# A hybrid mixer and gated ConvFFN layer: the up projection by seven products for eight, the output projection by quarters of the tokens

## The chip, the cores and the metric

One core of one Trainium2 chip. The metric is the time on the device of one execution, in microseconds (us), as the median of the runs. The engines are called by their names in the profile: PE (matrix products; PEld its weight loads), DVE (vector), ACT (scalar functions), POOL (GpSimd), SP (the queue that issues the DMAs).

## What is computed

One layer of a decoder for T = 1056 tokens: a prompt of 1024 and 8 samples of 4. The mixer takes the normalised input through one input projection into three groups of heads, and their outputs through one output projection; then comes the gated ConvFFN, whose two projections are half of the work. D = 1024 features, D_FF = 2816.

```python
def conv_ffn(h, ffn_state, w_up, conv_w, conv_b, w_down):
    up = jnp.einsum('bld,df->blf', h, w_up)
    gate, val = up[..., :D_FF], up[..., D_FF:]
    gate, new_state = causal_dwconv(gate, ffn_state, conv_w, conv_b)   # width 3, over the tokens
    out = jnp.einsum('blf,fd->bld', jax.nn.gelu(gate, approximate=True) * val, w_down)
    return out, new_state.astype(ffn_state.dtype)

# in the layer
    mix, ... = hybrid_mixer(rms_norm(x, norm_mix_pre), ...)   # ends with einsum('ble,ed->bld', mix, w_out)
    x = x + rms_norm(mix, norm_mix_post)
    f, nf = conv_ffn(rms_norm(x, norm_ffn_pre), ...)
    x = x + rms_norm(f, norm_ffn_post)
```

## The kernel before

Features lie on the 128 partitions, tokens along the free dimension. A dense product of one output tile (128 features) with a group of tokens runs over k, the tiles of 128 input features. To keep float32 accuracy with the fp32r type of PE, each operand is split into a rounded part and the rest (`h` and `l`), and each k takes three matmuls: `wh` with `xh`, `wh` with `xl`, `wl` with `xh`. `dense` issues them (`mm`, L203 in the profile). The tokens are taken in NG = 3 groups of G = 352.

`load_w` brings a weight tile: the DMA on SP (L263), the rounded part by ACT (L264), the rest by a subtraction on POOL (L265).

The order of the work. Tile's scheduler orders DVE, ACT, POOL and SP by priority; PE's order is written by hand: the class `Weave` draws steps from several streams, and the next step is that of the first stream whose operands should be there.

The stages, with their place in the profiled execution:

- The mixer for the prompt, to about 641 us.
- The samples and the output projection, to 814.7 us. `split_mix` makes the split operands of the mixer's outputs; `project` forms the 8 output tiles, first the two groups 0 and 1 for as long as the streams of the samples last, then the rest, then group 2. `finish` adds the input to the normalised result and makes the split operands of the FFN.
- The up projection, in five parts of the hidden tiles (`QUARTERS`). For a hidden tile `gate_conv` makes the gate: 3 groups x 8 k x 3 matmuls, each group's sums scaled out of PSUM by DVE (L303), then the convolution: ACT takes the middle tap with the bias (L212), DVE the two other taps by `scalar_tensor_tensor` over 1072 columns (L1682), ACT the gelu. `value` does the other half (DVE L303, the product with the gate L1695 to L1699) and splits the result into `hidh` (ACT, L1700) and `hidl` (DVE, L1701), which stay in SBUF.
- After each part `down` multiplies its hidden tiles into all 8 output tiles and adds them to `fa` in SBUF (DVE, L1732 and L1734). The last part is taken by groups, so that `final` (the norm, the residual and the output, L1748 to L1758) of a group runs beside the products of the next.

In the FFN five PSUM banks take the products in turn. A weight tile is loaded into one buffer (`w`), its parts into two pairs.

## Time and profile before

| what | value |
|---|---|
| runs | 1576.37, 1582.40 and 1576.41 us, median 1576.41 |
| span of the profiled execution | 1578.6 us (its time outside the profiler is not listed) |
| PE busy | 1496.2 us, 95% of the span |
| DVE, ACT, POOL busy | 920.7, 542.1, 546.1 us |
| mixer, 0 to 640 us | PE busy 587 us |
| samples and output projection, 640 to 815 us | PE busy 164 us |
| up and down projections, 815 to 1510 us | PE busy 695 us, without a gap |
| last group and output, 1510 to 1578.6 us | PE busy 50 us |

The span is the time from the first to the last instruction that the profiler saw. Matmuls overlap in the profile: each is shown for about 0.32 us, but one starts every 0.16 us, so that a time per matmul is taken from the starts, or from a stretch without gaps divided by its matmuls. "Idle before" is what an engine waited before an instruction, and the name behind the arrow what released it.

### The profile page before, as it was taken

To read this page: it belongs to the slowest core of one execution; us is meant where nothing else is said; L and a number is where in the kernel's file an instruction comes from. 1 tells how busy PE (TensorE), PEld (TensorE's weight loads), DVE (VectorE), ACT (ScalarE), POOL (GpSimd) and SP (SyncE) were. 2 spreads that over 40 slices of the span, in tenths; PEclk is the share of its full clock that TensorE was granted. 3 is DMA by queue.
4 is the path that set the end of the run, shared out by engine and by line. 5 is a ranking of instruction groups with operands and counts; after the bars stand their busy time and mean duration, and the time that the engine had idled before them with its cause. 6 is when DMAs were issued, how large, how long until landed. Compare 5 with 4: busy or idle time off the path is not lost.

```text
span 1578.6 us, 24157 instructions
## 1 busy us (share of the span) xinstructions
PE 1496.2 (95%) x9438; PEld 1453.1 (92%) x9438; DVE 920.7 (58%) x1818; ACT 542.1 (34%) x1173; POOL 546.1 (35%) x624
## 2 busy tenths in 40 slices
PE   8788999989999999999899999999999999999995
PEld 8788899879989989988889999999999999999994
DVE  6889888796474367636975522444245325424558
ACT  7644445443342232424652211221122112212353
POOL 6234433232354353566432122221222222122224
PEclk9989999999999999999999999999999999999997
DMA  5111010111111231324531112111111111111142
GB/s 180 43 48 30 23 45 25 34 32 30 43 55 47 79 112 47 102 76 152 187 100 41 44 42 62 41 41 42 52 54 34 41 61 42 40 55 54 52 151 110
DMA packets 51210, 100.63 MB, mean 64 GB/s; under 512 B 14857, under 2 KB 25737, under 8 KB 50713
## 3 DMA queue, kind: packets, MB, share of 16 engines
q1 hardware_dynamic: 51096, 99.10, 20.1%
q8 instruction: 74, 1.21, 0.3%
q14 instruction: 40, 0.32, 0.1%
HBM read 85.25 MB, written 13.31 MB: 62 GB/s over the span
## 4 chain that ended last, share of the span: by engine, by line
PE 63%; DVE 17%; ACT 6%; POOL 5%; issue 4%; DMA 4%; SPq 0%; DVEq 0%; POOLq 0%; ACTq 0%
PE acc L203 55%; PE mc L203 3%; PE mb L203 3%; DVE kq L465 2%; PE mb L207 2%; DMA E<-rows_dram 2%; POOL wl L265 1%; DVE hl L333 1%; DVE two L784 1%; DVE v L465 1%; ACT sq L212 1%; POOL E L868 1%; PE po L203 1%; DVE fs L344 1%; ACT E L212 1%
## 5 line engine op out<-in xcount | busy, mean ns | idle before, releaser
L203 PE MATMUL acc<-hh,wh 128*128 128x352 f32 x1952 | 660.7, 339 | 18.2 <-DVE pre L303 12.2
L203 PE MATMUL acc<-hh,wl 128*128 128x352 f32 x1960 | 635.8, 324 | 2.6 <-POOL wl L265 2.0
L203 PE MATMUL acc<-hl,wh 128*128 128x352 f32 x1952 | 631.9, 324 | 0.7 <-DVE hl L333 0.7
L203 PEld LDWEIGHTS acc<-hh,wh 128*128 128x128 f32 x1952 | 371.7, 191 | 25.3 <-DVE pre L303 8.5
L265 POOL TENSOR_TENSOR wl<-w,wh 128x1024 fp32r<-128x1024 f32 (+2 forms) x117 | 252.9, 2162 | 362.3 <-ACT wh L264 354.8
L203 PEld LDWEIGHTS acc<-hh,wl 128*128 128x128 f32 x1960 | 372.4, 190 | 4.2 <-POOL wl L265 2.3
L203 PEld LDWEIGHTS acc<-hl,wh 128*128 128x128 f32 x1952 | 373.0, 191 | 3.1 <-DVE hl L333 1.7
L264 ACT CAST wh<-w 128x1024 fp32r<-128x1024 f32 (+2 forms) x117 | 109.9, 939 | 416.4 <-PE acc L203 400.3
L203 PE MATMUL acc<-hidh,wh 128*128 128x352 f32 x444 | 143.8, 324 | 0.0
L203 PE MATMUL acc<-hidh,wl 128*128 128x352 f32 x444 | 143.3, 323 | 0.0
L203 PE MATMUL acc<-hidl,wh 128*128 128x352 f32 x444 | 143.2, 322 | 0.0
L303 DVE TENSOR_TENSOR fpre<-acc,rs 128x352 f32<-128x352 f32 (+1 forms) x88 | 35.8, 430 | 137.5 <-PE acc L203 135.1
L1734 DVE TENSOR_TENSOR fa<-fa,acc 128x352 f32<-128x352 f32 x96 | 49.8, 519 | 106.3 <-PE acc L203 105.9
L1682 DVE SCALAR_TENSOR_TENSOR fy<-fpre,vec,fy 128x1072 f32<-128x1072 f32 x44 | 79.3, 1802 | 36.7 <-ACT fy L212 36.0
L203 PEld LDWEIGHTS acc<-hidh,wh 128*128 128x128 f32 x444 | 83.4, 188 | 0.0
L203 PEld LDWEIGHTS acc<-hidl,wh 128*128 128x128 f32 x444 | 83.4, 188 | 0.0
L203 PEld LDWEIGHTS acc<-hidh,wl 128*128 128x128 f32 x444 | 83.4, 188 | 0.0
L1701 DVE TENSOR_TENSOR hidl<-hid,hidh 128x352 fp32r<-128x352 f32 x66 | 52.7, 799 | 37.8 <-ACT hidh L1700 37.8
L1677 POOL COPY ffn_o<-fpre 128x2 f32<-128x2 f32 x22 | 4.1, 186 | 157.8 <-DVE fpre L303 157.8
L465 DVE SCALAR_TENSOR_TENSOR kq<-pre,cw,kq 128x352 f32<-128x352 f32 (+1 forms) x72 | 53.4, 748 | 7.7 <-ACT kq L212 7.2
L1700 ACT CAST hidh<-hid 128x352 fp32r<-128x352 f32 x66 | 31.9, 483 | 74.2 <-DVE hid L1695 49.9
L303 DVE TENSOR_TENSOR hid<-acc,rs 128x352 f32<-128x352 f32 x66 | 34.4, 521 | 38.1 <-PE acc L203 38.1
(552 smaller groups left out, 2238.7 us busy)
## 6 DMA issues: line engine op xcount, KB each, us to landing
w<-in_w_up_dram SPq DMA_DIRECT2D x44, 512.0 KB
w<-in_w_in_dram SPq DMA_DIRECT2D x30, 512.0 KB
E<-rows_dram SPq DMA_DIRECT2D x24, 256.0 KB
w<-in_w_dn_dram SPq DMA_DIRECT2D x21, 256.0 KB
w<-in_w_out_dram SPq DMA_DIRECT2D x10, 512.0 KB
w<-in_w_dn_dram SPq DMA_DIRECT2D x16, 320.0 KB
xr<-in_xT_dram SPq DMA_DIRECT2D x24, 176.0 KB
hh<-x_dram SPq DMA_DIRECT2D x3, 1408.0 KB
```

The source lines that it names most:

```text
L203: return nc.tensor.matmul(out, **kw)
L207: return nc.tensor.transpose(out, in_, identity)
L212: i = nc.scalar.activation(**kw)
L264: nc.scalar.copy(out=wh[:, ks], in_=w[:, ks])
L265: gtt(out=wl[:, ks], in0=w[:, ks], in1=wh[:, ks].bitcast(F32), op=ALU.subtract)
L303: vtt(out=out, in0=ps, in1=r, op=ALU.mult)
L333: stt(out=hl[g][:, k, :], in0=x, scalar=col(vcol + k), in1=hh[g][:, k, :].bitcast(F32), op0=ALU.mult, op1=ALU.subtract)
L465: stt(out=y[:, a:b], in0=pre[:, a + j:b + j], scalar=cw2[:, 4 * t + j:4 * t + j + 1], in1=y[:, a:b], op0=ALU.mult, op1=ALU.add)
L1682: stt(out=y[:, :LF], in0=pre[:, j:j + LF], scalar=col(V_FW + 3 * f + j), in1=y[:, :LF], op0=ALU.mult, op1=ALU.add)
L1700: nc.scalar.copy(out=hidh[:, groups[g]], in_=hid)
L1701: vtt(out=hidl[:, groups[g]], in0=hid, in1=hidh[:, groups[g]].bitcast(F32), op=ALU.subtract)
L1734: vtt(out=fa[:, g, m, :], in0=fa[:, g, m, :], in1=ps[:, :G], op=ALU.add)
```

## The change

The tokens of the output projection and of the FFN are taken in NQ = 4 quarters of Q = 264.

The up projection. Two gate tiles of a pair (or two value tiles) and two quarters of tokens, with the input features in two halves of KH = 4 tiles, are a product of 2 x 2 blocks. It is formed by seven block products instead of eight (Winograd's form). The input sums are built once (`pieces`, on DVE, with the split by ACT and DVE); the weight sums are built for each pair by four DVE operations of 128x512 (`weights`), and each of the seven weight pieces is split by ACT and by POOL, or by DVE for p = 2 and 4 (`weight_piece`). The class `fast` is one pair, a task: product p of the two-quarter halves u = 0 and 1 is 4 k x 3 matmuls of 264 columns each. Products that belong to the same output are summed in one PSUM bank (1 and 2; 6, 7 and 4; 5 and 3), and what is shared between banks goes through SBUF (`f1`, `f6`, `f7`, L1872 and L1875). In a task's order, products 4 and 3 of the pair before stand between this pair's product 6 of u = 0 and its product 5. The first PLAIN = 4 gate tiles are done by plain products, since the input sums are not ready yet. Tasks: the value tiles 0 and 1, then by turns a gate pair and the value pair before it; 20 tasks in all.

The hidden tiles are written to DRAM (`hid_dram`) and read back for the down projection (`load_hid`), which now comes after the whole up projection, in six parts (`PARTS`, the first of one hidden tile alone), by quarters of tokens. The output projection takes quarters 0 and 1 beside the samples (`project_first`) and 2 and 3 after them (`project_last`). The weight buffer `w` has three places. PE's order is by hand to the end. The buffers of the mixer's normalised input become 16 tiles `h0` to `h15` over all tokens.

```diff
-QUARTERS = ((0, 5), (5, 10), (10, 14), (14, 18), (18, 22))
+Q = 264
+NQ = 4
+PLAIN = 4
+PARTS = ((0, 1), (1, 6), (6, 10), (10, 14), (14, 18), (18, 22))
...
+        def project_first():
+            for m in range(KD):
                 w = load_w(I["w_out"][m], KD)
-                for g in range(2):
-                    yield from product(m, w, g)
-                m += 1
-            yield lambda: not weave.streams[1:]
+                for q in range(2):
+                    yield from product(m, w, q)
+            for q in range(2):
+                weave.add(finish(q), 8)
+            have.add("half")
...
+            split_mix(2)
+            for m in range(3):
+                load(m)
+            split_mix(3)
+            for q in (2, 3):
+                for m in range(KD):
+                    yield from product(m, held[m], q)
+                    if q == 2 and m + 3 < KD:
+                        load(m + 3)
+                    if q == 3 and m < PLAIN:
+                        load_up(m)
+                weave.add(finish(q), 8)
+            have.add("projected")
...
+            def split(p, x):
+                hi, lo = (block(pool.tile([P, T], F32R, name=n)) for pool, n in places[p])
+                nc.scalar.copy(out=hi, in_=x)
+                vtt(out=lo, in0=x, in1=hi.bitcast(F32), op=ALU.subtract)
+                X[u][p] = hi, lo
...
+        def gate_task(i):
+            pres = [new_pre() for j in range(2)]
+            def out(j, h, u, x, ps):
+                gate_in(pres[j], 2 * u + h, x, ps)
+            def end():
+                ys[i] = [gate_conv(2 * i + j, pres[j]) for j in range(2)]
+            return fast(i, 0, out, end)
...
+                if x is not None:
+                    t = fo[0].tile([P, Q], F32, name="rs", bufs=2)
+                    vtt(out=t, in0=x, in1=ps, op=ALU.add)
+                    ps = t
+                for a, b, smp in quarter(q):
+                    o, p_, y = hids[j][:, q * Q + a:q * Q + b], ps[:, a:b], ys[i][j][:, q * Q + a:q * Q + b]
+                    if smp:
+                        o, p_ = (t.rearrange("p (b t) -> p b t", t=DS) for t in (o, p_))
+                        y = samp6(ys[i][j], SEQ + 2)[:, :, 0:DS]
+                    vtt(out=o, in0=y, in1=p_, op=ALU.mult)
...
+                    dma(out=hid_dram[2 * i + j], in_=hids[j])
+                ys.pop(i)
...
+            wh, wl = ring.pop(0)
+            nc.scalar.copy(out=wh, in_=x)
+            tt(out=wl, in0=x, in1=wh.bitcast(F32), op=ALU.subtract)
+            return wh, wl
...
+        class fast:
+            def __init__(self, i, val, out, end):
+                self.out, self.end = out, end
+                w = [wp.tile([P, KD, P], F32, name="w", bufs=3) for j in range(2)]
+                self.A = [[w[j][:, KH * r:KH * r + KH] for j in range(2)] for r in range(2)]
+                for r, j in ((0, 0), (1, 0), (1, 1), (0, 1)):
+                    dma(out=self.A[r][j], in_=I["w_up"][2 * (2 * i + r) + val][:, KH * j:KH * j + KH])
+                self.banks, self.sb, self.w = {}, {}, {}
+            def weights(self, p):
+                A = self.A
+                if p == 6:
+                    self.s = [fo[0].tile([P, KH, P], F32, name="ws", bufs=3) for j in range(2)]
+                    vtt(out=self.s[0], in0=A[1][0], in1=A[1][1], op=ALU.add)
+                    vtt(out=self.s[1], in0=self.s[0], in1=A[0][0], op=ALU.subtract)
+                elif p == 7:
+                    vtt(out=A[1][0], in0=A[0][0], in1=A[1][0], op=ALU.subtract)
+                elif p == 3:
+                    vtt(out=self.s[1], in0=A[0][1], in1=self.s[1], op=ALU.subtract)
+                x = {1: A[0][0], 2: A[0][1], 4: A[1][1], 7: A[1][0]}.get(p)
+                if x is None:
+                    x = self.s[p != 5]
+                return weight_piece(x, vtt if p in (2, 4) else gtt)
+            def run(self, p, u):
+                if p not in self.w:
+                    self.w[p] = self.weights(p)
+                wh, wl = self.w[p]
+                first = p in (1, 6, 5)
+                b = {1: 0, 2: 0, 6: 1, 7: 1, 4: 1, 5: 2, 3: 2}[p]
+                if first:
+                    self.banks[u, b] = (accr if b else accp).tile([P, 512], F32, name="acc")[:, :Q]
+                ps = self.banks[u, b]
+                xh, xl = X[u][p]
+                for k in range(KH):
+                    kw = dict(skip_group_check=not first)
+                    mm(ps, lhsT=wh[:, k, :], rhs=xh[:, k, :], start=first and k == 0, stop=False, **kw)
+                    mm(ps, lhsT=wh[:, k, :], rhs=xl[:, k, :], start=False, stop=False, **kw)
+                    mm(ps, lhsT=wl[:, k, :], rhs=xh[:, k, :], start=False, stop=k == KH - 1, **kw)
+                    yield 0
+                sb = self.sb
+                if p == 1:
+                    sb[u, 1] = fo[0].tile([P, Q], F32, name="f1", bufs=3)
+                    nc.scalar.copy(out=sb[u, 1], in_=ps)
+                elif p in (6, 7):
+                    sb[u, p] = fo[0].tile([P, Q], F32, name=f"f{p}", bufs=3 if p == 6 else 2)
+                    vtt(out=sb[u, p], in0=sb[u, 1], in1=ps, op=ALU.add)
+                    if p == 7:
+                        self.out(1, 1, u, sb[u, 7], self.banks[u, 2])
+                elif p == 2:
+                    self.out(0, 0, u, None, ps)
+                elif p == 4:
+                    self.out(1, 0, u, sb[u, 1], ps)
+                elif p == 3:
+                    self.out(0, 1, u, sb[u, 6], ps)
...
+            for q in range(NQ):
+                yield lambda: ("normed", q) in have
+                for f in range(PLAIN):
+                    ps = yield from dense(accr, held["up", f], operand, KD, q, Q)
+                    gate_in(pres[f], q, None, ps)
+                have.add(("plain", q))
...
+            prev = None
+            for n, (task, i) in enumerate(tasks):
+                cur = task(i)
+                if n == 0:
+                    for i in range(PLAIN // 2):
+                        ys[i] = [gate_conv(2 * i + j, pres[2 * i + j]) for j in range(2)]
+                for p, u in ((1, 0), (1, 1), (6, 0), (4, 0), (6, 1), (4, 1), (3, 0), (3, 1),
+                             (5, 0), (5, 1), (2, 0), (2, 1), (7, 0), (7, 1)):
+                    if p in (4, 3):
+                        if prev:
+                            yield from prev.run(p, u)
+                            if (p, u) == (3, 1):
+                                prev.end()
+                    else:
+                        yield from cur.run(p, u)
+                prev = cur
...
+        def load_hid(f, parts):
+            h, l = parts
+            dma(out=l.bitcast(F32), in_=hid_dram[f])
+            nc.scalar.copy(out=h, in_=l.bitcast(F32))
+            vtt(out=l, in0=l.bitcast(F32), in1=h.bitcast(F32), op=ALU.subtract)
+            return parts
...
+        for qi, (f0, f1) in enumerate(PARTS):
+            nf = f1 - f0
+            n = KD if qi == 0 else KD // nf
+            after = []
+            todo = list(range(PARTS[qi + 1][1] - f1)) if qi < last else []
+            if qi < last:
+                for m in range(KD):
+                    if m % n == 0:
+                        ws = first if qi == 0 else down_w(qi, m, n)
+                    for q in range(NQ):
+                        down(m, ws[m % n], q, qi, hid)
+                        if todo and (qi == 0 or q == 0):
+                            after.append(new_hid(qi + 1, todo.pop(0)))
+                hid = after
```

### How the order moves

PE, one pair of the up projection. Names: `hh0` to `hh2` are the operands of the three groups. Before, one tile takes its 24 matmuls for group 0, then those for groups 1 and 2, each group into a bank of its own:

```order
L203 MATMUL acc_10588<-hh0_7760,wh_10583 128x352
L203 MATMUL acc_10588<-hl0_7761,wh_10583 128x352
L203 MATMUL acc_10588<-hh0_7760,wl_10584 128x352
...
L203 MATMUL acc_10618<-hh1_7904,wh_10583 128x352
...
L203 MATMUL acc_10648<-hh2_8178,wh_10583 128x352
```

Now, in a gate task in the middle of the up projection, the first matmul of each of its first eight products (p,u), which are (1,0), (1,1), (6,0), then (4,0) of the pair before, (6,1), then (4,1), (3,0) and (3,1) of the pair before; 11 more matmuls follow each:

```order
L206 MATMUL acc_10596<-h0_7826,wh_10547 128x264
...
L206 MATMUL acc_10611<-h8_8325,wh_10547 128x264
...
L206 MATMUL acc_10634<-n0_8409,wh_10630 128x264
...
L206 MATMUL acc_10380<-n6_8522,wh_10630 128x264
...
L206 MATMUL acc_10666<-r0_8647,wh_10630 128x264
...
L206 MATMUL acc_10412<-h4_8738,wh_10630 128x264
...
L206 MATMUL acc_10492<-h5_7900,wh_10697 128x264
...
L206 MATMUL acc_10505<-h13_8605,wh_10697 128x264
```

Of the five banks `accr`, four are held by the pair before and `acc_10634` is the fifth; `acc_10666` is the bank that `acc_10380` leaves. Behind the products shown come (5,0), (5,1), (2,0), (2,1), (7,0) and (7,1), then the next task.

DVE, the convolution of a gate. Before, it stands between the sums of its own tile and those of the next, value tile (`rs` are the norm's factors):

```order
L303 TENSOR_TENSOR fpre_13556<-acc_13559,rs0_8079 128x352
L303 TENSOR_TENSOR fpre_13556<-acc_13585,rs1_8166 128x352
L303 TENSOR_TENSOR fpre_13556<-acc_13611,rs2_8257 128x320
L303 TENSOR_TENSOR fpre_13556<-acc_13611,rs2_8257 128x8x4
L1682 SCALAR_TENSOR_TENSOR fy_13640<-fpre_13556,vec_75,fy_13640 128x1072 x2
L303 TENSOR_TENSOR hid_13678<-acc_13653,rs0_8079 128x352
L1695 TENSOR_TENSOR hid_13678<-fy_13545,hid_13678 128x352
L1701 TENSOR_TENSOR hidl0_13646<-hid_13678,hidh0_13645 128x352
```

Now two gates' convolutions (four operations: both gates' first taps, then both second) stand between the outputs of product 3 and of product 2, and the next task's first weight sums (`ws`) behind the outputs of products 2 and 7:

```order
L1773 SCALAR_TENSOR_TENSOR fy_11454<-fpre_11078,vec_75,fy_11454 128x1072
L1773 SCALAR_TENSOR_TENSOR fy_11463<-fpre_11079,vec_75,fy_11463 128x1072
...
L1805 TENSOR_TENSOR n10_8895<-fy_10962,acc_11328 128x264
L1805 TENSOR_TENSOR n10_8895<-fy_10962,acc_11343 128x264
L1875 TENSOR_TENSOR f7_11547<-f1_11341,acc_11364 128x264
L1841 TENSOR_TENSOR ws_11610<-w_11572,w_11573 128x512
L1798 TENSOR_TENSOR rs_11549<-f7_11547,acc_11476 128x264
L1875 TENSOR_TENSOR f7_11564<-f1_11356,acc_11396 128x264
L1805 TENSOR_TENSOR n11_8896<-fy_10971,rs_11549 128x264
L1798 TENSOR_TENSOR rs_11566<-f7_11564,acc_11489 128x264
L1842 TENSOR_TENSOR ws_11611<-ws_11610,w_11572 128x512
```

What moved: four long operations together instead of two, with the weight sums queued on the same engine behind the outputs that follow.

DVE, the first part of the down projection. Before, its copies from PSUM (`fa`) follow the hidden tiles that DVE just made, with nothing else between them:

```order
L1697 TENSOR_TENSOR hid_9246<-fy_9049,hid_9246 128x320
L1699 TENSOR_TENSOR hid_9246<-fy_9049,hid_9246 128x32
L1701 TENSOR_TENSOR hidl4_9154<-hid_9246,hidh4_9153 128x352
L1732 COPY fa_9252<-acc_9259 128x352
```

Now the first part's 32 copies have the splits of the next part's five reloaded hidden tiles between them:

```order
L1798 TENSOR_TENSOR rs<-f_13629,acc 128x264
L1805 TENSOR_TENSOR n_8893<-fy,rs 128x232
L1805 TENSOR_TENSOR n_8893<-fy,rs 128x32
L1967 COPY fa<-acc 128x264 x12
L1946 TENSOR_TENSOR hidl_13880<-hidl_13880,hidh_13879 128x1056
L1967 COPY fa<-acc 128x264
L1946 TENSOR_TENSOR hidl_13890<-hidl_13890,hidh_13889 128x1056
L1967 COPY fa<-acc 128x264
L1946 TENSOR_TENSOR hidl_13900<-hidl_13900,hidh_13899 128x1056
```

What moved: the products of one hidden tile alone (32 groups of 3 matmuls) stand before those that need five reloaded tiles.

## Rows read from the trace of the kernel before

**Rows 1.** Windows by stage: us, PE, PEld, DVE, ACT, POOL busy, PEclk, DMA share, GB/s.

```profile
core 0 of [0], span 1578.6 us
...
760.00:815.00 55.00, 45.56 (x238) 42.27 (x238) 47.99 (x79) 32.61 (x68) 20.40 (x16) 0.91 0.46 147
815.00:1510.00 695.00, 695.00 (x4350) 695.00 (x4350) 296.53 (x445) 150.06 (x189) 165.20 (x165) 1.00 0.16 51
...
1558.00:1579.00 21.00, 2.79 (x5) 1.12 (x4) 16.28 (x24) 3.22 (x6) 9.74 (x9) 0.56 0.36 137
```

**Rows 2.** Chain of waits, its longest piece: start us, us, what.

```profile
814.71 694.66 PE acc L203 x4344
```

**Rows 3.** Waits of PE, 760 to 815 us: us in total, times, longest.

```profile
PE acc L203 <- ACT mix L1571: 3.3, 1, 3.3
PE acc L203 <- POOL wl L265: 2.0, 1, 2.0
...
PE acc L203 <- ACT wh L264: 1.0, 1, 1.0
```

**Rows 4.** Timeline of PE's weight loads where products are short: start us, us.

```profile
682.27 0.41 PEld L203 LDWEIGHTS mc<-kqG,hh 128*128 128x128 f32 x3 [0.24 <-issue]
...
682.60 0.19 PEld L203 LDWEIGHTS acc<-hh,wh 128*128 128x128 f32 x1
```

**Rows 5.** Lines by form, 900 to 1500 us: busy us, mean ns, idle before.

```profile
L1682 DVE SCALAR_TENSOR_TENSOR fy<-fpre,vec,fy 128x1072 f32<-128x1072 f32 x34 | 62.8, 1846 | 27.8 <-ACT fy L212 27.2
...
L303 DVE TENSOR_TENSOR hid<-acc,rs 128x352 f32<-128x352 f32 x51 | 26.6, 521 | 31.9 <-PE acc L203 31.9
...
L265 POOL TENSOR_TENSOR wl<-w,wh 128x512 fp32r<-128x512 f32 x17 | 23.2, 1366 | 85.8 <-ACT wh L264 85.8
L212 ACT ACTIVATE fy<-fpre,vec 128x1072 f32<-128x1072 f32 x17 | 21.8, 1281 | 0.0
...
L264 ACT CAST wh<-w 128x512 fp32r<-128x512 f32 x17 | 10.6, 621 | 65.2 <-PE acc L203 65.2
...
L303 DVE TENSOR_TENSOR fpre<-acc,rs 128x320 f32<-128x320 f32 x17 | 8.4, 492 | 56.2 <-PE acc L203 56.2
```

**Rows 6.** Timeline of all engines, a bank's release in the mixer.

```profile
50.48 0.32 PE L203 MATMUL acc<-hh,wl 128*128 128x352 f32 x1
...
50.83 0.51 DVE L303 TENSOR_TENSOR raw<-mc,rs 128x352 f32<-128x352 f32 x1
...
51.76 0.57 DVE L303 TENSOR_TENSOR li<-acc,rs 128x320 f32<-128x320 f32 x2
...
52.45 0.19 PEld L203 LDWEIGHTS acc<-hh,wh 128*128 128x128 f32 x1 [1.93 <-issue]
52.48 0.40 PE L203 MATMUL acc<-hh,wh 128*128 128x352 f32 x1 [1.67 <-DVE li L303]
```

**Rows 7.** Lines by form, 640 to 830 us, the convolution's taps.

```profile
L1682 DVE SCALAR_TENSOR_TENSOR fy<-fpre,vec,fy 128x1072 f32<-128x1072 f32 x4 | 5.3, 1334 | 4.1 <-ACT fy L212 4.0
```

**Rows 8.** Timeline, DVE with two SBUF operands beside POOL.

```profile
758.10 2.52 POOL L265 TENSOR_TENSOR wl<-v,wh 128x1024 fp32r<-128x1024 f32 x1
...
758.27 3.16 DVE L1630 TENSOR_TENSOR mix<-mix,xr 128x352 f32<-128x352 f32 x2
```

**Rows 9.** Timeline of PE after a wait, 764 to 771 us.

```profile
765.19 0.66 PE L203 MATMUL acc<-hh,pre 128*128 128x352 f32 x1 [3.29 <-ACT mix L1571]
...
768.92 0.32 PE L203 MATMUL acc<-hl,pre 128*128 128x352 f32 x1
```

**Rows 10.** Windows of 5 us, columns as in rows 1.

```profile
765.00:770.00 5.00, 4.81 (x20) 4.82 (x21) 5.00 (x10) 3.85 (x9) 1.59 (x1) 0.66 0.59 181
...
785.00:790.00 5.00, 3.84 (x16) 3.84 (x16) 3.87 (x5) 1.38 (x3) 3.19 (x3) 0.66 0.41 125
```

**Rows 11.** The page, section 2: what the DMAs moved, in 40 slices of the span.

```profile
GB/s 180 43 48 30 23 45 25 34 32 30 43 55 47 79 112 47 102 76 152 187 100 41 44 42 62 41 41 42 52 54 34 41 61 42 40 55 54 52 151 110
```

**Rows 12.** Timeline of PE, the end.

```profile
1563.50 1.54 PE L203 MATMUL po<-fs,ones 128*128 128x352 f32 x2 [5.42 <-DVE fs L344]
```

More of the change, by code (lines that the diff above doesn't have):

```diff
@@ L77 @@
 KS = (4, 5, 6, 7, 0, 1, 2, 3)
-LAST = 3
 B16 = 16
@@ L344, in square_sum, with sums @@
             (gtt if len(ss) > 1 and k % 2 == 0 else vtt)(out=ss[i % len(ss)], in0=ss[i % len(ss)], in1=sq, op=ALU.add)
-    def sums(pool, name, n=2):
-        return [pool.tile([P, G], F32, name=f"{name}{i}") for i in range(n)]
+    def sums(pool, name, n=2, w=G):
+        return [pool.tile([P, w], F32, name=f"{name}{i}") for i in range(n)]
     order = ExitStack()
@@ new lines, in new_operand, with split_mix, product @@
+        def new_operand(q):
+            t = [block(hnp.tile([P, T], F32R, name=f"h{4 * q + i}")) for i in range(4)]
+            ops[q] = t[:2], t[2:]
+        def split_mix(q):
+            new_operand(q)
+            for i in (1, 0):
+                split_quarter(q, i, q == 0)
+        def product(m, w, q):
+            if m == 0:
+                sqs[q] = on.tile([P, 2, Q], F32, name="ss", bufs=4)
+            ps = yield from dense(accp, w, operand, KS, q, Q)
+            act(out=mix[m][:, quarters[q]], in_=ps[:, :Q], func=AF.Copy, scale=col(V_NPOST + m))
+            if m % 2 == 0:
+                sqs[q, 0] = sqs[q] if m == 0 else on.tile([P, 2, Q], F32, name="sq", bufs=2)
+            act(out=sqs[q, 0][:, m % 2, :], in_=ps[:, :Q], func=AF.Square)
+            if m % 2 and m > 1:
+                vtt(out=sqs[q], in0=sqs[q], in1=sqs[q, 0], op=ALU.add)
@@ L1642 @@
+        onstack = ExitStack()
+        on = onstack.enter_context(tc.tile_pool(name="on", bufs=1, side="right"))
+        smp_done = lambda: all(x + " samples" in have for x in ("gdn", "ml", "ssd"))
+        with tc.tile_pool(name="smp", bufs=1) as smp:
+            log_tables()
             samples(smp)
@@ new lines, with up @@
+        ys, hid4 = {}, []
+        def up():
+            yield lambda: "projected" in have
+            pres = [new_pre() for f in range(PLAIN)]
+            for q in range(NQ):
[4 more added lines that the diff above has]
+                have.add(("plain", q))
+            yield lambda: "pieces" in have
+            hid4.extend(fn.tile([P, T], F32, name=f"n{8 + j}") for j in range(4))
+            ffn_io["st"] = fo[0].tile([P, NF, 16], F32, name="st_ffn")
+            ffn_io["out"] = fo[0].tile([P, NF, 18], F32, name="ffn_o")
+            dma(out=ffn_io["st"], in_=I["st_ffn"])
+            tasks = [(value_task, 0)]
+            for i in range(PLAIN // 2, NF // 2):
+                tasks += [(gate_task, i), (value_task, i - 1)]
+            tasks.append((value_task, NF // 2 - 1))
+            prev = None
[11 more added lines that the diff above has]
+                                prev.end()
+                    else:
+                        yield from cur.run(p, u)
+                prev = cur
+            for p, u in ((4, 0), (4, 1), (3, 0), (3, 1)):
+                yield from prev.run(p, u)
+            prev.end()
+            dma(out=O["ffn"], in_=ffn_io["out"])
@@ new lines @@
+        weave.add(project_last(), 9)
+        weave.add(make_pieces(), 8)
+        weave.add(up(), 10)
+        weave.run(lambda: not weave.streams)
+        fo = fo[0]
+        hid0 = [fo.tile([P, 1074], F32R, name="fy", bufs=4)[:, :T] for x in "hl"]
+        upper.close()
+        low.close()
+        fp = ph.enter_context(tc.tile_pool(name="fp", bufs=1))
+        ssum = [sums(fp, f"fs{q}", 1, Q) for q in range(NQ)]
+        fa = fp.tile([P, NQ, KD, Q], F32, name="fa")
+        count = [0] * NQ
@@ new lines, in down @@
+        def down(m, w, q, qi, hid):
+            nf = len(hid)
+            ps = drain(dense(accr, w, lambda k, q: [t[:, quarters[q]] for t in hid[k]], nf, q, Q))
+            if qi == 0:
+                nc.vector.tensor_copy(out=fa[:, q, m, :], in_=ps[:, :Q])
+            else:
+                vtt(out=fa[:, q, m, :], in0=fa[:, q, m, :], in1=ps[:, :Q], op=ALU.add)
+            if qi == last:
+                if q == NQ - 1 and count[q] == KD - 1:
+                    ssum[q].append(fp.tile([P, Q], F32, name="sq1", bufs=2))
+                    act(out=ssum[q][1], in_=fa[:, q, m, :], func=AF.Square)
+                else:
+                    square_sum(fp, fa[:, q, m, :], ssum[q], count[q])
+                count[q] += 1
@@ new lines @@
+                ws = {}
+                for q in range(NQ):
+                    for m in range(KD):
+                        if q == 0 and m % n == 0:
+                            parts = None
+                            if m >= 2 * n:
+                                parts = [tile_w(fp.tile([P, T], F32R, name=f"hid{x}{m // n - 2}", bufs=2)) for x in "hl"]
+                            ws.update(zip(range(m, m + n), down_w(qi, m, n, parts)))
+                        down(m, ws[m], q, qi, hid)
+                        if m:
+                            next(rest, None)
+                    rest = chain(rest, final(q))
```

414 lines of the change are left out of this document (200 added, 214 removed).

## The prediction

> **What bounds the kernel now.** I read the windows by stage first [rows 1]. The reader is to see the line from 815 to 1510 us: PE and its weight loads are busy for all 695.00 us at the full granted clock (1.00, the 2.4 GHz level), DVE for 296.53, POOL for 165.20. The chain of waits says the same as one piece: 694.66 us with 4344 matmuls and nothing between [rows 2]. So the up and down projections cost what their matmuls cost, 694.66 / 4344 = 0.1599 us each, and every wait put into this stage is new time. The stage before it differs: from 760 to 815 us PE is busy for 45.56 of 55.00 us, and its waits there are on single evictions and weight pieces [rows 3]. The last 21 us belong to DVE. The sum below is made against the span of the profiled execution, 1578.6 us; that lies 2.2 above the median of the runs, 1576.4, and I take the difference off at the end. About 0.5%, 7.9 us, can be told from no change.
>
> **The matmuls.** Before, the up projection has 44 tiles x 3 groups x 24 = 3168 matmuls of 352 columns, the output projection 576, the down projection 1584. Now the up projection has 4 plain gate tiles x 4 quarters x 24 = 384 and 20 tasks x 14 products x 12 = 3360, together 3744, of 264 columns; the others have 768 and 2112. What a matmul of 264 columns takes no row shows. At full clock 352 columns are 146.7 ns, so 13.2 ns of the 159.9 are beside the columns. If these stay as they are, 264 columns take 110.0 + 13.2 = 123.2 ns; if all shrinks with the columns, 119.9; if the 128 columns of the weights share the time with the 352, 159.9 x 392 / 480 = 130.6. The weight loads alone are no higher floor: where products are short, three loads start in 0.33 us, one per 0.11 [rows 4]. I take 123.2, since nothing in the rows lets a fixed part shrink, and keep the other two for the range.
> Up: 3744 x 0.1232 - 3168 x 0.1599 = 461.3 - 506.6 = -45.3. Output projection +2.5, down projection +6.9. Together **-35.9** (-57.7 and +13.1 at the bounds).
> The Trainium skill ("TensorE: Matmul & The Clock Gate", section "Back-to-back issue gap") gives N / 2.4 + 2.5 ns for one matmul behind another. By it the 352 columns would take 149.2 ns, which the chain's 159.9 does not bear out; with 112.5 at 264 columns the three terms would be -49.6 instead of -35.9.
>
> **One bank too few for product 6.** In every task but the first, (6,1) takes the bank that (4,0) of the pair before leaves, and (4,0) stands just ahead of it on PE. Before, no product waits for a bank in this stage. Now DVE must read the bank in between. A DVE eviction takes 521 ns for 352 columns and 492 for 320 [rows 5]; that is 0.906 ns a column, so 0.44 us for 264. Around it, from a release in the mixer [rows 6]: the last matmul is shown for 0.32 us, 0.16 longer than the spacing; DVE starts 0.03 behind its end; the next weights load 0.12 behind the eviction's end (51.76 + 0.57 to 52.45) and the first product runs some 0.08 longer. 0.16 + 0.03 + 0.44 + 0.12 + 0.08 = 0.83, and 0.03 more for the product behind it: 0.86 x 19 = **+16.3**. If DVE has half an operation queued, it is 2 us each and 38; if nothing is exposed, 0.
>
> **The convolution queue.** For each of the 9 gate pairs DVE does four taps over 1072 columns in a row. I follow it from the end of product (3,1), t = 0; a product is 12 x 0.1232 = 1.48 us. Its last outputs leave DVE at 0.8. ACT still has a cast ahead (0.62) and then 1.28 for the middle tap [rows 5]: 2.8. DVE starts at 3.8, since POOL's subtraction of a piece (1.37, rows 5) stands in its way: two DVE operations on two SBUF operands took 3.16 us beside one of POOL's of 2.52 [rows 8]. Four taps at 1.334, the mean of the shortest group [rows 7], end at 9.15. Then comes the output of (2,0), 9.6; its bank is what the next task's (1,0) needs, due at 6 x 1.48 = 8.87 and now starting at 9.83: 0.96 late. Behind the taps stand nine operations up to the second weight sum (seven of 0.44, two of 512 columns at 521 + 160 x 0.906 = 666 ns): 13.57. The piece for product 6 then needs ACT (0.62) and POOL (1.37): 15.56. PE has done (1,0) and (1,1) by 9.83 + 2.96 = 12.79 and waits 2.77. Together 3.73 x 9 = **+33.6**. With taps at the mean of the whole stage, 1.846, it is 2.05 more each; with the sums ready in time, 0. The value pairs' tasks have no taps and I cost their queue at nothing: their DVE operations lie under 14 products, 20.7 us, and would show as waits of (6,0) if not.
>
> **The clock behind such waits.** After the wait of 3.29 us the next 13 matmuls start over 3.73 us instead of 2.08 [rows 9], and the five microseconds there show a granted clock of 0.66; the five that hold the wait of 2.0 us [rows 3] show 0.66 too [rows 10]. That is the lower level, 1.2 GHz, for some 3.4 us, and 1.65 us lost. Behind a wait of 1.67 us the next product takes 0.40 us [rows 6], against 0.66 behind the one of 3.29: no fall there. A wait of 2.77 belongs with the former: 9 x 1.65 = **+14.9**. Below, 0.
>
> **Smaller terms.** At the first task the taps of the four plain gates, eight operations, stand ahead of the first outputs: +3 (0 to 10.7, their whole length). At the start of the down projection the single hidden tile gives PE 96 x 0.1232 = 11.8 us of work, but DVE has 32 copies of 0.44 and five splits of reloaded tiles, 128x1056, at about 1.3 [rows 7]: 20.6; and the five reloads are 2.7 MB, 18 us at the 147 GB/s of [rows 1] (some slices reach 187 [rows 11]). So PE waits some 8, and one fall of the clock comes to it: +9.6 (5 to 15). Samples and projection: before, PE lacks 9.4 of the 55 us to 815 and runs at a clock of 0.91 [rows 1]; now the other quarters' products can stand beside `finish`, but those of quarter 2 wait for the samples' end: -2.5 (-9 to +5). The end: DVE's operations have 264 columns instead of 352, and the wait of 5.42 us before the last norm [rows 12] shrinks by a quarter with a part of what follows: -2 (-5 to 0). At the start two weight loads now go ahead of the last input loads: +1 MB at 180 GB/s [rows 11], 5.8 at most, +1 taken.
>
> **Sum.** -35.9 + 16.3 + 33.6 + 14.9 + 3 + 9.6 - 2.5 - 2 + 1 = +38.0: a span of 1616.6, and 1614.4 against the median. The hidden tiles' way through DRAM while the up projection runs costs nothing by itself, since the queues carry 51 GB/s there [rows 1].
>
> **The rivals.**
> *The queues stay under PE's work* (faster). If the taps start early, or the weight sums of the next pair are done before them, PE never waits for product 6's piece, and the bank's wait is half. It decides at the end of (1,1): the piece must be done 2.8 us sooner than in my walk. For it: DVE is busy for 43% of this stage and the walk puts one late step on another. Against it: the order of DVE, where the sums stand behind taps and outputs. -35.9 + 8.2 + 3 + 8 - 2.5 - 2 + 1 = -20.2: 1556; with 119.9 ns a matmul, 1534.
> *Short waits that leave the clock up* (no change). 1.5 us for each gate pair, no fall: -35.9 + 16.3 + 13.5 + 3 + 8 - 2.5 - 2 + 1 = +1.4: 1578.
> *Taps beside POOL* (slower). All taps at 1.846: +18.4, 1633. For it: that is the mean before; against it: POOL's operations are half as long here.
> *The weights' columns count* (slower). 130.6 ns a matmul: +49, 1663. Against it: the loads hide under products of this length [rows 4].
> That the change does not save columns is excluded by the counts: 5328 x 352 against 6624 x 264, 126,720 fewer.
>
> **The numbers.** My forecast 0.40, no change 0.16, queues covered 0.22, covered and 119.9 ns 0.08, taps beside POOL 0.08, weights' columns 0.06. So faster 0.30, same 0.16, slower 0.54. The forecast's own range is 1592 (119.9 ns with all waits) to 1633. The whole range, 1545 to 1645, leaves out the covered case at the lower price and the shared columns.
>
> **What would show it.** The chain's matmuls in the up projection at 0.123 us each; 19 waits of (6,1) on DVE (L1798 or L1759), under 1 us; nine waits of over 2 us on the weight piece (L1822) with a granted clock under 1.00 behind them; a stretch of some 8 us of waits on L1946 at the start of the down projection. It is wrong if PE's busy share between the first and the last task is above 98%, or if the matmuls start more than 0.128 us apart where nothing waits.

## The result, and the profile after

The changed kernel takes 1633.35 us (median of four runs, 1629.08 to 1635.91) against 1576.56 before: 1.0355 times the time, interval 1.033 to 1.0379. The forecast was 1614 and slower; the range, 1545 to 1645, held it. The span of its profiled execution is 1631.9 us, 53.3 more than before. The page and the chain of waits of the changed kernel:

```profile
span 1631.9 us, 27483 instructions
...
PE 1483.9 (91%) x10756; PEld 1432.3 (88%) x10756; DVE 1024.0 (63%) x2039; ACT 618.6 (38%) x1332; POOL 568.5 (35%) x653
```

```profile
898.56 20.65 PE acc L206 x168
...
987.01 4.49 PE acc L206 x22
992.00 20.66 PE acc L206 x168
1013.18 11.94 PE acc L206 x96
1025.16 6.62 issue
...
1033.88 2.95 PE acc L206 x22
1037.33 20.66 PE acc L206 x168
...
1313.89 14.87 PE acc L206 x120
...
1353.84 206.10 PE acc L206 x1677
```

PE is busy for 12 us less and the program is 53 us longer. The last piece, 1677 matmuls in 206.10 us, would make 122.9 ns each, but its first 33 matmuls, up to 1360.57, ran mostly at the lower clock (a granted clock of 0.59, below); the 1644 behind them took 199.37 us, 121.3 ns each, and that is the price where nothing waits. But the one unbroken piece of 694.66 us [rows 2] has become a pattern: in each pair of tasks 168 matmuls, 96, then breaks. The waits of PE in the up projection, and in the stretch of the samples and the output projection (us in total, times, longest):

```profile
PE acc L206 <- POOL wl L1822: 14.2, 9, 1.6
PE acc L206 <- ACT wh L1821: 6.0, 9, 0.7
PE acc L206 <- DVE rs L1798: 5.9, 10, 1.2
PE acc L206 <- DVE fpre L1759: 4.7, 9, 0.5
```

```profile
PE acc L206 <- DVE h L1579: 9.7, 2, 9.2
PE acc L206 <- ACT ss L215: 7.0, 1, 7.0
PE acc L206 <- ACT sq L215: 6.8, 1, 6.8
PE po L206 <- DVE ss L1622: 6.3, 1, 6.3
```

The nines are the nine gate pairs: product 6's weight piece (L1821, L1822), and the bank of (6,1) behind a value pair (L1798, ten times) or a gate pair (L1759). The second list, which goes on with shorter waits, was not forecast. The windows by stage answer to [rows 1]: from 700 to 815 us PE is busy for 83.06 of 115 us, at a clock of 0.85 and 0.87.

```profile
700.00:760.00 60.00, 39.98 (x250) 33.77 (x249) 44.13 (x45) 28.74 (x53) 27.22 (x16) 0.85 0.47 158
760.00:815.00 55.00, 43.08 (x303) 41.70 (x303) 31.71 (x27) 27.00 (x53) 7.74 (x3) 0.87 0.29 104
```

One convolution queue, in the order that the prediction walked through. DVE and POOL first, then PE (start us, us):

```profile
928.16 5.90 DVE L1773 SCALAR_TENSOR_TENSOR fy<-fpre,vec,fy 128x1072 f32<-128x1072 f32 x4 [1.80 <-ACT fy L215]
933.98 0.76 DVE L1805 TENSOR_TENSOR n<-fy,acc 128x264 f32<-128x264 f32 x2
934.66 0.41 DVE L1875 TENSOR_TENSOR f<-f,acc 128x264 f32<-128x264 f32 x1
935.00 0.68 DVE L1841 TENSOR_TENSOR ws<-w 128x512 f32<-128x512 f32 x1
935.60 0.41 DVE L1798 TENSOR_TENSOR rs<-f,acc 128x264 f32<-128x264 f32 x1
...
936.97 0.68 DVE L1842 TENSOR_TENSOR ws<-ws,w 128x512 f32<-128x512 f32 x1
...
938.58 0.68 DVE L1844 TENSOR_TENSOR w<-w 128x512 f32<-128x512 f32 x1
```

```profile
938.37 4.94 POOL L1822 TENSOR_TENSOR wl<-ws,wh 128x512 fp32r<-128x512 f32 x3 [9.18 <-ACT wh L1821]
```

```profile
938.35 0.51 PE L206 MATMUL acc<-n,wh 128*128 128x264 f32 x2 [0.67 <-ACT wh L1821]
940.44 0.59 PE L206 MATMUL acc<-n,wl 128*128 128x264 f32 x1 [1.58 <-POOL wl L1822]
...
943.38 0.40 PE L206 MATMUL acc<-n,wh 128*128 128x264 f32 x2
```

The four taps end at 934.06, the second weight sum at 937.65; PE waits for ACT's cast and then for POOL, whose first piece comes at 940.4, 2.0 us after its start instead of the 1.3 that POOL takes alone; DVE's next sum (938.58) runs in that time. Behind that, 13 matmuls start over 2.94 us (940.44 to 943.38) where 1.58 is the rule: the lower clock, 1.36 us lost.

The clock does not fall behind each of these breaks. All nine are alike, 0.67 and 1.58 us, yet it fell behind five and stayed up behind four. Two of them, in stretches of 5 us from the start of (6,0) (the third number from the end is the granted clock):

```profile
984.90:989.90 5.00, 3.40 (x17) 3.19 (x18) 3.11 (x4) 1.01 (x2) 4.94 (x3) 0.77 0.30 107
1031.80:1036.80 5.00, 3.42 (x24) 3.01 (x24) 3.00 (x4) 0.97 (x2) 4.96 (x3) 1.00 0.32 105
```

In the chain above these are the 22 matmuls that take 4.49 us and the 22 that take 2.95: a fall costs 1.54 us. A pair of tasks lasts 46.87 us with a fall and 45.33 without, 46.15 on average. In the three runs below that leave the up projection as it is, it fell behind five, four and five of the nine. Why behind some and not behind others of the same length no run shows.

### The profile page after: what moved, and what is told of

The parts are those of the page before. It is cut to its first block, busy times and chain, and to the rows that moved or that the text cites. A ratio compares the mean times of both kernels' runs of the same rounds, so it can differ in the third digit from the quotient of the medians.

```text
span 1631.9 us, 27483 instructions
## 1 busy us (share of the span) xinstructions
PE 1483.9 (91%) x10756; PEld 1432.3 (88%) x10756; DVE 1024.0 (63%) x2039; ACT 618.6 (38%) x1332; POOL 568.5 (35%) x653
## 4 chain that ended last, share of the span: by engine, by line
PE 59%; DVE 18%; issue 8%; ACT 6%; POOL 5%; DMA 3%; SPq 0%; DVEq 0%; POOLq 0%; ACTq 0%
PE acc L206 50%; PE mb L206 3%; PE mc L206 3%; DVE kq L469 2%; PE mb L210 2%; DMA E<-rows_dram 2%; POOL wl L1822 1%; PE po L206 1%; DVE two L788 1%; DVE v L469 1%; DVE fa L1987 1%; ACT E L215 1%; POOL E L872 1%; DVE xf L1988 1%; DVE pre L306 1%
## 5 line engine op out<-in xcount | busy, mean ns | idle before, releaser
L206 PE MATMUL acc<-h,wh 128*128 128x264 f32 (+1 forms) x3040 | 681.8, 315 | 26.5 <-DVE pre L306 11.6
L206 PEld LDWEIGHTS acc<-h,wh 128*128 128x128 f32 x3040 | 499.9, 192 | 36.1 <-DVE h L1579 10.6
L206 PE MATMUL acc<-h,wl 128*128 128x264 f32 (+1 forms) x1528 | 468.0, 306 | 0.2 <-POOL wl L615 0.2
L206 PEld LDWEIGHTS acc<-h,wl 128*128 128x128 f32 x1528 | 292.3, 191 | 0.8 <-POOL wl L615 0.8
L206 PE MATMUL acc<-hidh,wl 128*128 128x264 f32 x608 | 173.6, 286 | 4.1 <-POOL wl L1960 4.1
L206 PE MATMUL acc<-hidh,wh 128*128 128x264 f32 x608 | 174.0, 286 | 0.0
L206 PE MATMUL acc<-hidl,wh 128*128 128x264 f32 x608 | 173.6, 285 | 0.0
L1822 POOL TENSOR_TENSOR wl<-ws,wh 128x512 fp32r<-128x512 f32 x60 | 91.1, 1532 | 168.4 <-ACT wh L1821 168.3
L270 POOL TENSOR_TENSOR wl<-w,wh 128x1024 fp32r<-128x1024 f32 x41 | 100.3, 2446 | 112.1 <-ACT wh L269 97.1
L206 PE MATMUL acc<-n,wh 128*128 128x264 f32 x640 | 127.0, 295 | 6.0 <-ACT wh L1821 6.0
L1960 POOL TENSOR_TENSOR wl<-w,wh 128x1024 fp32r<-128x1024 f32 (+1 forms) x23 | 49.7, 2159 | 177.8 <-ACT wh L1959 174.8
L206 PEld LDWEIGHTS acc<-n,wh 128*128 128x128 f32 x640 | 104.7, 199 | 7.9 <-ACT wh L1821 7.9
L1821 ACT CAST wh<-w 128x512 fp32r<-128x512 f32 x80 | 47.7, 619 | 141.1 <-PE acc L206 81.6
L1822 POOL TENSOR_TENSOR wl<-w,wh 128x512 fp32r<-128x512 f32 x40 | 57.8, 1445 | 95.4 <-ACT wh L1821 83.6
```

Of the source, the lines that this page charges most:

```text
L206: return nc.tensor.matmul(out, **kw)
L270: tt(out=wl[:, ks], in0=w[:, ks], in1=wh[:, ks].bitcast(F32), op=ALU.subtract)
L1821: nc.scalar.copy(out=wh, in_=x)
L1822: tt(out=wl, in0=x, in1=wh.bitcast(F32), op=ALU.subtract)
L1960: gtt(out=wl, in0=w, in1=wh.bitcast(F32), op=ALU.subtract)
```

## The experiments

All edits are made to the changed kernel. Twelve runs: first single causes, then sums of them. What an edit gains is told as the difference of the medians; the kernel before, timed beside the runs, took 1574.3 to 1577.8 us, so that some 3 us between two runs say nothing.

**Product (6,1) behind (4,1).**

```diff
-(1, 0), (1, 1), (6, 0), (4, 0), (6, 1), (4, 1), (3, 0), (3, 1),
+(1, 0), (1, 1), (6, 0), (4, 0), (4, 1), (6, 1), (3, 0), (3, 1),
```

> Edit: product (4,1) of the pair before goes ahead of (6,1), so that 12 matmuls (1.48 us) stand between (4,0) and the product that needs its bank. Theory (each wait costs what its own queue costs): the 19 waits on L1798 and L1759, 10.6 us in the changed kernel, vanish, with some 0.15 us each of slow start: 13 us less, 1620. Rival (PE is held by DVE's total, the wait only changes its place): the waits appear again at (6,0) or (5,0) of the same task and the time stays within 4 us of 1633.

1613.05 us, 20 less. L1798 and L1759 are gone from PE's waits, and only nine waits of 0.2 us came in their place. The chain of this kernel:

```profile
1068.18 35.00 PE acc L206 x286
...
1112.14 36.41 PE acc L206 x286
```

A pair of tasks behind which the clock stays up went from 45.33 us to 43.96. That is 12 us in nine, for waits of 9.4 (the tenth on L1798, 1.2 us, lies ahead of them); each break also costs some 0.2 to 0.3 us of slow start behind it, a little more than the theory's 0.15. The rest the theory did not have: the clock now falls behind two of the nine breaks at (6,0) instead of five (36.41 us for 286 matmuls above, 35.00 elsewhere), though those breaks are as long as before, and three falls are 4.6 us. Why it falls less often is not shown.

**Product 6's piece on DVE.**

```diff
-                return weight_piece(x, vtt if p in (2, 4) else gtt)
+                return weight_piece(x, vtt if p in (2, 4, 6) else gtt)
```

> Edit: the subtraction of product 6's weight piece on DVE instead of POOL. Theory: POOL's late start is the last step of the chain to (6,0); the nine waits on L1822 of 1.58 us become some 0.5, the whole wait then stays under 1.7 us and the granted clock stays up behind it: 10 us of waits and 10 us of clock less, 1613. Rival (the clock falls for any break at that place): waits 10 us less but the slow matmuls behind (6,0) remain: 1623. Second rival (DVE's queue only grows): no change, 1633.

1611.70 us, 22 less, where the theory with the clock said 1613 and the one without it 1623. The same place as above, in this kernel:

```profile
933.79 0.51 PE L206 MATMUL acc<-n,wh 128*128 128x264 f32 x2 [0.66 <-ACT wh L1821]
934.76 0.39 PE L206 MATMUL acc<-n,wl 128*128 128x264 f32 x1 [0.46 <-DVE wl L1822]
```

The wait is 0.46 instead of 1.58, and the matmul behind it 0.39 instead of 0.59: the clock did not fall here, nor behind any of the nine. A pair of tasks takes 44.20 us, 1.13 less than one without a fall before. So of the 22 us 10 are the waits and 7.7 the five falls, 17 to 18 together; the other 4 lie ahead of the first task (872.95 us instead of 876.80), where the edit changes nothing.

**The second gate's taps a task later.**

```diff
-                ys[i] = [gate_conv(2 * i + j, pres[j]) for j in range(2)]
+                ys[i] = [gate_conv(2 * i, pres[0])]
+                later.append(lambda: ys[i].append(gate_conv(2 * i + 1, pres[1])))
```

> Edit: the convolution of a pair's second gate is issued a task later; in DVE's order three taps instead of four now stand ahead of the second weight sum. Theory (the queue of taps makes the sum late): the piece for product 6 comes 1.48 us sooner, the waits of 0.67 and 1.58 us in each of the nine gate pairs shrink to about 0.8 together and the clock stays up: 13 us of waits and 8 us of clock less, 1612. Rival (DVE only shifts the delay, the tap now stands ahead of the sums for products 7 and 3): waits of the same size there, 1627 or more.

1631.69 us: nothing. The rival was right as to the mechanism, though the place was another: the wait of (6,0) on the piece vanished, and the bank of (6,1) took it over, 25.2 us in ten waits instead of 5.9.

```profile
937.22 0.39 PE L206 MATMUL acc<-n,wl 128*128 128x264 f32 x1 [0.16 <-POOL wl L1823]
942.82 0.76 PE L206 MATMUL acc<-r,wh 128*128 128x264 f32 x2 [2.68 <-DVE rs L1799]
```

DVE's scheduler put three taps first and the fourth behind the second sum, and there it stands ahead of the eviction.

**Output projection: a buffer, a tile, the order.** Three runs. The sums of the second norm kept in `sx`:

```diff
-            s = on.tile([P, 2, Q], F32, name="ss", bufs=4)
+            s = sx[:, 0:2]
```

> Edit: the sums for the second norm stay in the tile sx, so that the tile ss is never reused. Theory: the squares of the first output tile of quarter 2 wait for a buffer that the norm of quarter 1 still holds, and with them the bank: the wait of 7.0 us on the squares goes, with one fall of the clock: 8 us less, 1625. Rival (ACT has too much to do in that stretch): the wait moves to the next eviction, within 3 us of 1633.

1629.81 us. Quarters 2 and 3 swapped in the tiles:

```diff
-            t = [block(hnp.tile([P, T], F32R, name=f"h{4 * q + i}")) for i in range(4)]
+            t = [block(hnp.tile([P, T], F32R, name=f"h{4 * (0, 1, 3, 2)[q] + i}")) for i in range(4)]
```

> Edit: quarters 2 and 3 of the mixer's outputs change places in the tiles h8 to h15, so that quarter 2's operands do not lie where the last sample state is still being written out. Theory (the output DMA holds the tile): the 9.2 us wait on the split of quarter 2 (L1579) shrinks to about 4: 5 us less, 1628. Rival (DVE's queue of splits and weight subtractions holds it): 9 us of waits stay, 1633.

1630.06 us. Both are some 3 us below the changed kernel's median and inside the spread of its runs, so neither is a measured gain. Both waits went as the theories said, and both came back one step on: without the buffer's wait of 7.0 us the norm's product waits twice, for 12.1 us instead of 6.3; with the tiles swapped the 9.2 us on L1579 became 2.3 and the norm's product waits for 13.1.

Then both edits, with the norms' products later in PE's order and the evictions ahead on ACT:

```diff
-f_rows=12500, f_wait=4500
+f_rows=22000, f_wait=9000
...
+            with tc.high_priority(offset=300):
                 act(out=mix[m][:, quarters[q]], in_=ps[:, :Q], func=AF.Copy, scale=col(V_NPOST + m))
```

> Edits in the output projection alone: second norm's products 9.5 us and first norm's 4.5 us later in PE's order, sums kept in sx, quarters 2 and 3 swapped in h8 to h15, evictions of the products ahead of the norms on ACT. Theory (PE's order puts a norm's product in front of work that is ready, and then each link of the chain norm, eviction, split is waited for): PE's waits between 730 and 860 us, 31 us in the changed kernel, fall to about 12, with three falls of the clock fewer: 24 us less, 1609. Rival (DVE has too much to do from 735 to 775 us in any order): the waits come back at the splits of the next quarters, 1627 or more.

1622.46 us: 11 less, half of what the theory said. The norm's product now waits 1.1 us, but some of the wait came back at the splits, the squares and the first task, in part as the rival had it. One place shows what holds DVE there (DVE, then POOL, of this kernel):

```profile
775.99 6.20 DVE L1634 TENSOR_TENSOR mix<-mix,rstd 128x1056 f32<-128x1056 f32 x2 [0.53 <-ACT rstd L317]
```

```profile
775.20 5.88 POOL L271 TENSOR_TENSOR wl<-w,wh 128x1024 fp32r<-128x1024 f32 x2 [24.80 <-ACT wh L270]
```

Two such operations took 2.43 us in the changed kernel where POOL was idle; here POOL's two subtractions of the next weights cover them.

**The sums.** The first three edits together:

> Edits: the three of the up projection together (product 4 of u = 1 ahead of (6,1), product 6's piece on DVE, second gate's taps a task later). If the queues' costs are separate, they add up: 20 us (measured alone), 22 us (measured alone), and 8 us of what is left at (6,0): 1583. If they were the same microseconds: 1600 or more.

1596.69 us, 37 less than the changed kernel, where 50 was expected and the first two alone would add up to 42. A pair of tasks takes 42.80 us, and 45.33 - 1.37 - 1.13 is 42.83: the two edits add up, the falls of the clock can be saved only once, and the taps gave nothing here either. With the output projection's edits, the down projection's first copies shared with ACT and its last weight pieces on DVE:

> Edits: those three, those of the output projection, the first down part's copies shared between DVE and ACT, and the late weight pieces of the last part on DVE. Theory (the seven products pay if the waits go): 1583 less 24 for the projection, 6 for the wait of 4.1 us and its clock in the last part, 3 for the copies: 1550, below the kernel before by 1.6%. Rival (waits only change place): not below 1576.

1581.93 us, 1.0028 times the kernel before (1.001 to 1.0046), where 1550 was expected. The waits that stayed in the up projection were again the bank of (6,1), 11.9 us. So the taps were put back, and the weight sums moved instead:

```diff
+                    with tc.high_priority(offset=60):
                         vtt(out=self.s[0], in0=A[1][0], in1=A[1][1], op=ALU.add)
                         vtt(out=self.s[1], in0=self.s[0], in1=A[0][0], op=ALU.subtract)
```

> Edits in the up projection: product (4,1) ahead of (6,1), product 6's piece on DVE (both measured alone, 20 and 22 us), and the next task's two weight sums and that piece ahead of the outputs of product 7 in DVE's order, taps left where they were. Theory (what is left at (6,0) is the nine operations that stand ahead of the second sum): the waits of 0.67 and 0.46 us at (6,0) go in all nine gate pairs, 10 us more than the first two edits: 1633 - 20 - 22 - 10 = 1581. Rival (as with the moved tap, DVE hands the delay on): the wait comes back at the bank of (6,1) or at (1,0), 1592 or more.

1599.95 us, where 1581 was expected: 33 less than the changed kernel, and the first two edits alone come to 42, so the earlier sums by themselves gave nothing. The waits at (6,0) are gone in all pairs but one; the wait returned at the bank, 11.5 us in nine. This time the rows show why (POOL, DVE and PE of this kernel):

```profile
936.54 3.15 POOL L1822 TENSOR_TENSOR wl<-ws,wh 128x512 fp32r<-128x512 f32 x2 [9.17 <-DVE rs L1798]
```

```profile
937.04 2.69 DVE L1805 TENSOR_TENSOR n<-fy,rs 128x232 f32<-128x232 f32 x2
```

```profile
941.67 0.51 PE L206 MATMUL acc<-r,wh 128*128 128x264 f32 x2 [1.39 <-DVE rs L1798]
```

The two products with the gate, which take 0.49 us in the changed kernel, last 2.69 beside POOL's two subtractions, and all behind them on DVE is late. The same edits were also joined with those of the other stages, with all weight pieces of the projection stretch on DVE, and once with the second norms later still:

> Those edits, and in the output projection those of the run before it (order of the norms on PE, sums in sx, tiles swapped, evictions first on ACT, here with more priority) with the weight pieces of that stretch on DVE instead of POOL; the first down part's copies shared with ACT; the last part's late pieces on DVE. Theory (POOL's subtractions hold DVE's two-operand work up in that stretch, and ACT behind it): 1581 - 11 (measured for the projection's edits) - 8 (POOL out of the way) - 5 (down projection) = 1557, below the kernel before by 1.2%. Rival (DVE is full there, and four more subtractions make it fuller): 1570.

> The same with the second norms' products another 8 us later in PE's order. Theory (PE's order waits for the chain of the norms): 3 us less than the kernel beside it. Rival (the norms must be done before the first plain tiles anyway): the waits come later, at the splits, and the time is the same or 3 us more.

1573.84 us (0.9975 times before, 0.996 to 0.999) and 1572.89 (0.9972, 0.9955 to 0.9989). The first was expected at 1557; the 11.5 us at the bank were still in it. The later norms changed nothing that can be measured. Last, products 3 and 5 joined those whose piece DVE subtracts:

```diff
-                return weight_piece(x, vtt if p in (2, 4, 6) else gtt)
+                return weight_piece(x, vtt if p in (2, 3, 4, 5, 6) else gtt)
```

> The same as the kernel with the later second norms, and two more weight pieces (products 3 and 5) subtracted on DVE instead of POOL. Theory (behind the taps POOL's subtraction of those pieces holds DVE's product with the gate for 2 us, and with it the eviction that (6,1) waits for): the nine waits of 1.3 us on L1800 fall to under 0.3: 10 us less, 1563, 0.9% below the kernel before. Rival (DVE itself is the limit there): the waits stay, with another name, and the time is 1573 or more.

**1557.92 us, 0.9894 times the kernel before (0.987 to 0.9917): the fastest of all.** PE's waits from 850 to 1330 us, and the chain of waits there:

```profile
PE acc L207 <- ACT fa L1971: 4.7, 2, 4.3
PE acc L207 <- DVE f L1879: 2.6, 1, 2.6
```

```profile
915.14 41.12 PE acc L207 x336
956.29 41.12 PE acc L207 x336
```

A pair of tasks is now 336 matmuls in 41.12 us, 122.4 ns each, without a wait. The same place, DVE and POOL of this kernel, and the busy times of the kernel without and with the last edit:

```profile
919.46 0.50 DVE L1807 TENSOR_TENSOR n<-fy,rs 128x232 f32<-128x232 f32 x2
```

```profile
925.44 1.29 POOL L1824 TENSOR_TENSOR wl<-w,wh 128x512 fp32r<-128x512 f32 x1 [15.66 <-ACT wh L1823]
```

```profile
PE 1462.9 (93%) x10756; PEld 1416.8 (90%) x10756; DVE 1041.2 (66%) x2053; ACT 621.9 (40%) x1348; POOL 504.2 (32%) x623
...
PE 1465.1 (94%) x10756; PEld 1420.6 (91%) x10756; DVE 1036.4 (66%) x2093; ACT 621.5 (40%) x1348; POOL 452.6 (29%) x583
```

POOL is idle for 15.66 us there, and the two products with the gate take 0.50 us again instead of 2.69. DVE does 40 operations more and is busy for 5 us less.

## Why the prediction was right, and where it was not

- **The matmuls**: 121.3 ns against the 123.2 taken; the part beside the columns shrank too, from 13.2 to 11.3 ns. 6624 x 0.1213 - 5328 x 0.1599 is -48.5, forecast -35.9. The Trainium skill's gap ("TensorE: Matmul & The Clock Gate", section "Back-to-back issue gap"), which the page itself calls that of an isolated matmul, gives 112.5 ns at 264 columns and 149.2 at 352; the trace, with 121.3 and 159.9, does not agree. That the sum by it, -49.6, lies beside the -48.5 is chance: its two prices are low by 8.8 and 10.7 ns, and over 6624 and 5328 matmuls that cancels.
- **Bank, queue and clock in the up projection**: forecast 16.3 + 33.6 + 14.9 = 64.8. The nine pairs take 415.33 us (898.56 to 1313.89), 46.15 each; less 336 x 0.1213 that is 5.4 each, 48.5. All three mechanisms were there, in their places, and each was undone in a run, the queue only in a sum. The bank cost 14 by the run that undid it, near its forecast. The walk's step that was too dear is DVE's queue: operations behind one another start every 0.34 us (264 columns) and 0.60 (512), while the sum took 0.44 and 0.67, the time that each is shown for. With taps that end 0.6 us sooner, (1,0) is 0.13 late instead of 0.96, and (6,0) waits 0.67 + 1.58 instead of 2.77. The clock's term is half: five falls of 1.54 us, 7.7, where nine of 1.65 were forecast.
- **Start of the down projection**: forecast 9.6, measured 14.5: from 1334.42 to 1360.57 for 96 matmuls that need 11.6 us. PE's waits on L1967 are 7.9 of it; most of the rest is the lower clock, 0.59 in the last stretch. The cause was only in part as forecast: the first copy waits for the hidden tiles' writes to DRAM, whose SBUF the sums `fa` take over, and then four copies wait for the splits of L1946, 0.87 us each time on PE.

```profile
1334.42 0.41 PE L206 MATMUL acc<-fy,wh 128*128 128x264 f32 x2
...
1360.57 0.28 PE L206 MATMUL acc<-hidh,wh 128*128 128x264 f32 x1
```

```profile
1340.31 2.65 DVE L1967 COPY fa<-acc 128x264 f32<-128x264 f32 x7 [3.24 <-DMA hid_dram<-n]
```

```profile
1353.80:1361.00 7.20, 7.16 (x37) 7.16 (x38) 5.67 (x15) 1.57 (x3) 0.00 (x0) 0.59 0.69 284
```

- **The last part**: no term; a wait of 4.1 us on a weight piece of POOL (L1960) behind two others, and the lower clock behind it (0.55 from 1565.7 to 1572 us), together some 7.
- **The end**: forecast -2; from the last product to the end 20.8 us before and 18.7 now. The wait before the last norm, which was to shrink from 5.42 us, is 5.94; what follows it got shorter.
- **Samples and output projection**: this step failed. "The other quarters' products can stand beside `finish`": -2.5, between -9 and +5. With the terms above the 53.3 us leave some 34 for this stage, the mixer's start, the plain tiles and the first tasks, where 1.5 was forecast. PE's listed waits are 36.5 us from 600 to 860 us, against 12.4 from 600 to 815 before. The remaining 10 or so fit the lower clock (0.85 and 0.87 above, 0.91 before), but were not taken apart. The chain was not walked: the split behind the last states' DMA (9.2), the norm's product that PE's order puts next (6.3), the squares behind the norm on ACT (7.0 and 6.8). Two edits took the first and the third of these away, and the wait came back a step later; with PE's and ACT's order changed as well they brought 11 us.

That the total came within 19 us is luck: the matmuls and the up projection's queues were put 29 us too dear, and the output projection with the start and the last part of the down projection some 44 too cheap (the rest of the 19 is the step from span to median, which lay 2.2 below the span before and 1.5 above it now). Two rivals that named nearly the measured time were no nearer to the cause. "Taps beside POOL" said 1633, with taps of 1.846 us; four taps took 5.90, 1.48 each. The rival in which the queues stay under PE's work is no property of the change as made; the last run shows that it can be had, but its 1557.92 against that rival's 1556 is chance too: it has none of the bank's 8.2 us that the rival kept, and some 15 us of waits in the output projection that the rival did not have.

What stays open: why the output projection's stage still waits for some 15 us in the best kernel (splits and norms of quarters 2 and 3), why the clock fell behind some breaks and not behind others of the same length, and how much of the 14.5 us at the start of the down projection could go; a place for `fa` apart from the hidden tiles was not tried.

## What to carry to other kernels

When arithmetic is traded for shorter matmuls and more vector work, walk every queue that feeds the matrix engine from one period to the next; here a saving of 48 us went into breaks of 0.5 to 1.6 us and the falls of the clock behind them, and the output projection's new order cost some 30 more. A wait taken away is a gain only if the next instruction on that engine is ready: the moved taps and the swapped tiles moved the wait, while in sum a reordered product, earlier weight sums, subtractions on the right engine and the edits of the other stages brought the program 1.1% below the kernel before. Where a break leads to a fall of the clock, shortening it can pay twice: 10 us of waits and 7.7 of clock went with product 6's piece on DVE.

## What was not expected of the hardware

A DVE operation on two SBUF operands waits out a subtraction on POOL: 2.69 us instead of 0.49, and moving two of POOL's pieces to DVE took some 12 us from the program (0.9894 against 0.9972 times before), although DVE had more to do. The Trainium skill ("SBUF — State Buffer", section "SBUF: two separate sides") says that a DVE operation with two SBUF inputs and an operation of POOL that reads SBUF share a pair of ports, and that the one that starts first holds it for its whole instruction; the trace agrees, with the two durations above. The size of the effect was the surprise, since POOL was busy for only 35% of the changed kernel's span.

A wait of 0.66 us and, two products on, one of 0.46 left the clock up behind all nine gate pairs of that run; 0.67 and then 1.58 let it fall behind five of nine in the changed kernel and behind two of nine with the bank's waits gone. Neither of the two is as long as the 1.67 us behind which it stayed up before [rows 6].
